# Index scores and the top-256 search two query tiles ahead, and their room reused for score rows

## The chip, the cores and the metric

The kernel runs on one core of a Trainium2 chip. The metric is the device time of one execution in microseconds (us). The engines are TensorE (PE in the profile, its weight loads PEld), VectorE (DVE), ScalarE (ACT), GpSimd (POOL) and SyncE (SP), which issues most of the DMA transfers.

## What is computed

One transformer block on 1024 tokens of width 1024: a hybrid attention, an attention to 256 memory rows, and a squared-ReLU MLP of width 4096. The hybrid attention has eight heads of dense-sparse attention (DSA), in which every query attends only to the 256 keys that an index network scores highest, and eight heads of NSA with three branches (compressed, selected, window). Cut to what the change touches:

```
idx_score = einsum('bqhs,bqh->bqs', relu(einsum('bqhd,bsd->bqhs', qi, k_i)), wi)   # 8 index heads
idx_score = where(pos <= t, idx_score, -inf)
_, sel = top_k(idx_score, 256)
s = einsum('bqhd,bqkd->bhqk', qd, k_d[sel]) * scale        # DSA: softmax over the selected keys
o_dsa = softmax(s) @ v_d[sel]
o_nsa = o_cmp * g0 + o_slc * g1 + o_win * g2               # NSA, three softmax attentions
x = x + concat(o_dsa, o_nsa) @ w_out
x = x + memory_attention(rms_norm(x));  x = x + relu(rms_norm(x) @ w_ff_in)**2 @ w_ff_out
```

The kernel does not gather the 256 keys. It finds the 256th largest index score of every query row, and adds a mask of 0 or 1e30 to the DSA scores.

## The kernel before

The 1024 queries are eight tiles of 128 rows. The program is written as Python generators, which yield after each step an amount of work `w` in the planner's own units; a scheduler then fixes the order of the instructions on every engine when the program is built, with semaphores between the engines. Each engine executes its own list in that order.

There are two streams. The **fill** (`fill`, L1100) is the projection of the second half of the tokens (`project`, part 1), the memory rows (`memory`), output projection and memory attention for tiles 0 and 1 and then 2 and 3 (`between`), the MLP of tiles 0 to 3 (`mlp`), and `between` for tiles 4 and 5. `between` reads the attention outputs of its tiles, which `finish` (L713) stored to DRAM. The **attention** (`attend`, L835) walks the query tiles t = 0 to 7. `together` (L110) merges the two: fill is taken while its sum stays under the attention's sum times a pace (1.35, later 1.75); a stage of the fill that needs the outputs of tile n is held until the attention's tile is past n; and where `attend` yields `(t, None)`, the attention is held until the next half of the projection is out, with fill alone meanwhile.

In one tile, NSA and DSA come as units: `scores` (L667) for two heads, one unit ahead of `values` (L697). `scores` puts two score matmuls into PSUM ("S", two buffers), DVE adds the mask and copies to a score row `S` in SBUF (L686), ACT takes the exponential (L688), POOL normalizes (L693). `values` transposes the row on PE (L703), ACT and DVE split it in two parts (L235, L236), and PE multiplies by V (psPV). A tag `S` has NS = 4 rows of 4 KB a partition.

`index_mask` (L600) makes the mask of one tile beside the attention of the tile before it: `beside` (L89) interleaves `tile_work(t)` with the index work in proportion. First come the index scores: for eight heads two matmuls into PSUM "S", a ReLU on ACT into `ir` (L612), a weighted sum on DVE into `isc` (L616, L618). Then the search, 32 rounds on ACT alone, each round three instructions that need each other's result:

```python
for b in range(15, -1, -1):                                   # for the high and the low 16 bits
    s.activation(mask, src, AF.Sign, bias=c, accum_out=over)  # L644: over the whole row, and the sum of it
    s.activation(step, over, AF.Sign, bias=nd)                # L645
    s.activation(c, step, AF.Identity, scale=-0.5 * (1 << b), bias=c)   # L646
    yield 0.1
```

and at its end some ten DVE instructions that make the mask (L650 to L663). `isc`, `tkh` and `tkl` have one buffer each, so the index scores of the next tile cannot be written until the search before is through. `attend` runs it one tile ahead: `index_mask(aw, st, t + 1)` in tile t; tiles 0 and 1 need no mask, so there are six searches, of tiles 2 to 7, beside tiles 1 to 6. The index keys of tiles 4 to 7 come from part 1 of the projection, so the hold for it stands before the first tile whose index work reads them.

`q_prep` (L560) loads a head group's queries from DRAM (`qin`, one DMA on SP's queue, L564), normalizes and rotates them on POOL and DVE, transposes and splits them.

Of the kernel before, what the change touches and what calls it, by code (L numbers as in the profile page):

```python
# [9 lines left out]
F32 = mybir.dt.float32  # L10
F32R = mybir.dt.float32r
# [11 lines left out]
P = 128  # L23
L = 1024
# [64 lines left out]
def beside(ga, ta, gb, tb):  # L89

    da = db = 0.0
    la = lb = True
    while la or lb:
        if la and (not lb or da * tb <= db * ta):
            w = next(ga, None)
            la = w is not None
            da += w or 0.0
        else:
            w = next(gb, None)
            lb = w is not None  # L100
            db += w or 0.0
        if w is not None:
            yield w
# [63 lines left out]
def build(nc, tc, I, C, out):  # L167
# [41 lines left out]
    def swap(x):  # L209
        return halves(x)[..., ::-1, :]  # L210

    def halves(x):
        if len(x.shape) == 2:
            return x.rearrange("p (j i) -> p j i", j=2)
        return x.rearrange("p h (j i) -> p h j i", j=2)
# [4 lines left out]
    def small(pool, tag, w, dt=F32, bufs=2, p=P):  # L220
        return pool.tile([p, w], dt, tag=tag, name=tag, bufs=bufs)
# [128 lines left out]
    nc.sync.dma_start(qg[:, 1, :], row(W["nsa_qn_g"]).to_broadcast([P, 64]))  # L350
    nc.sync.dma_start(qg[:, 2, :], W["nsa_kn_g"][0:1].to_broadcast([P, 64]))
    v.tensor_scalar(qg[:, 0:2, :], qg[:, 0:2, :], -1.0, None, op0=ALU.mult)
    qgs = at.tile([P, 3, 64], F32, tag="qgs", name="qgs")
    v.tensor_copy(halves(qgs), swap(qg))
    xqg = bcast("xqg", row(W["xq_norm_g"]), 128)
    masks = const16("c_masks", [P, 640])
    window, causal = masks[:, 0:512], masks[:, 128:640]
# [10 lines left out]
    def project(pool, part, pe, st):  # L368
# [17 lines left out]
        nc.sync.dma_start(ctab[:, 0, :], C["c_ccos"])  # L386
        nc.sync.dma_start(ctab[:, 1, :], C["c_csin"])
        v.tensor_tensor(ctab[:, 0, :], ctab[:, 0, :], qg[:, 2, :], op=ALU.mult)
        v.tensor_tensor(ctab[:, 1, :], ctab[:, 1, :], qgs[:, 2, :], op=ALU.mult)
        kg = ring(pool, "pc", [P, 8, 64])  # L390
        lnb = kg[:, 6, :]
        for h, src in enumerate([W["nsa_kn_g"][1:2], W["nsa_kn_g"][1:2], W["nsa_kn_g"][2:3], W["nsa_kn_g"][2:3],
# [164 lines left out]
    def part_of(t):  # L557
        return max(i for i, (a, _) in enumerate(PARTS) if a <= t)

    def q_prep(aw, t, kind, hg):  # L560

        q = small(aw, "qin", 256, bufs=1).rearrange("p (h d) -> p h d", d=64)
        part = part_of(t)
        nc.sync.dma_start(q, qraw[kind][part][hg][:, t - PARTS[part][0], :].rearrange("p (h d) -> p h d", d=64))  # L564
        ta = small(aw, "qta", 256, bufs=1).rearrange("p (h d) -> p h d", d=64)
        tb = small(aw, "qtb", 256, bufs=1).rearrange("p (h d) -> p h d", d=64)
        if kind == 2:
            A, B = cos[:, t, None, None, :].to_broadcast([P, 4, 2, 32]), sin[:, t, :]
        else:
            tab = small(aw, "qtab", 128, bufs=1).rearrange("p (a d) -> p a d", d=64)  # L570
            g.tensor_tensor(halves(tab[:, 0, :]), halves(qg[:, kind, :]), cos[:, t, None, :].to_broadcast([P, 2, 32]), op=ALU.mult)
            g.tensor_tensor(tab[:, 1, :], sin[:, t, :], qgs[:, kind, :], op=ALU.mult)
            A, B = halves(tab[:, 0, :])[:, None, :, :].to_broadcast([P, 4, 2, 32]), tab[:, 1, :]
            s.activation(ta, q, AF.Square)
            ss, r = small(aw, "qss", 4), small(aw, "qr", 4)
            v.tensor_reduce(ss, ta, axis=AX.X, op=ALU.add)
            g.tensor_scalar(ss, ss, 64 * EPS, None, op0=ALU.add)
            g.tensor_tensor(r, ss, mhalf[:, 0:1].to_broadcast([P, 4]), op=ALU.pow)
            g.tensor_tensor(q, q, r[:, :, None].to_broadcast([P, 4, 64]), op=ALU.mult)
        g.tensor_tensor(halves(ta), halves(q), A, op=ALU.mult)  # L580
        v.tensor_tensor(halves(tb), swap(q), halves(B)[:, None, :, :].to_broadcast([P, 4, 2, 32]), op=ALU.mult)
        qd = small(aw, "qd", 512, bufs=1).rearrange("p (h b d) -> p h b d", h=4, b=2)
        v.tensor_tensor(qd[:, :, 0, :], ta, tb, op=ALU.add)
        g.tensor_tensor(qd[:, :, 1, :], ta, tb, op=ALU.add)
        own = ("iqh", "iql", 1) if kind == 2 else ("qh", "ql", 2)
        qh = aw.tile([P, 4, P], F32R, tag=own[0], name=own[0], bufs=own[2])
        ql = aw.tile([P, 4, P], F32R, tag=own[1], name=own[1], bufs=own[2])
        p2 = pst("PT", [P, 4, P])
        for h in range(4):
            te.transpose(p2[:, h, :], qd[:, h, :, :].rearrange("p b d -> p (b d)"), ident)  # L590
        split_ps(p2, qh, ql)
        return qh, ql
# [4 lines left out]
        a = (n + 1) // 2  # L597
        return [(0, a), (a, n - a)]

    def index_mask(aw, st, t):  # L600
        Wd = (t + 1) * P
        acc = small(aw, "isc", L, bufs=1)
        for hg in range(2):
            qh, ql = q_prep(aw, t, 2, hg)
            for h in range(4):
                for c, n in chunks_of(t + 1):
                    sp = pst("S", [P, n * P])
                    mv = st["K"][:, IDX, c * P:(c + n) * P]
                    mm(sp, qh[:, h, :], mv, True, False)
                    mm(sp, ql[:, h, :], mv, False, True)  # L610
                    r = small(aw, "ir", 512)
                    s.activation(r[:, :n * P], sp, AF.Relu)  # L612
                    dst = acc[:, c * P:(c + n) * P]
                    w = st["wi"][:, t, hg * 4 + h:hg * 4 + h + 1]
                    if hg == 0 and h == 0:
                        v.tensor_scalar(dst, r[:, :n * P], w, None, op0=ALU.mult)  # L616
                    else:
                        v.scalar_tensor_tensor(dst, r[:, :n * P], w, dst, op0=ALU.mult, op1=ALU.add)  # L618
                yield 0.15 * (t + 1)
        sc = acc[:, :Wd]  # L620
        v.tensor_tensor(acc[:, t * P:Wd], acc[:, t * P:Wd], causal[:, 384:512], op=ALU.subtract)
        bits = sc.bitcast(I16).rearrange("p (n b) -> p n b", b=2)
        mask = small(aw, "dmask", L, BF16)[:, :Wd]
        sgn = mask.bitcast(I16)
        hi, lo = small(aw, "tkh", L, U16, 1)[:, :Wd], small(aw, "tkl", L, U16, 1)[:, :Wd]
        v.tensor_scalar(sgn, bits[:, :, 1], 0.0, -1.0, op0=ALU.is_lt, op1=ALU.mult)
        v.scalar_tensor_tensor(hi.bitcast(I16), sgn, -32768, bits[:, :, 1], op0=ALU.bitwise_or, op1=ALU.bitwise_xor)
        v.tensor_tensor(lo.bitcast(I16), bits[:, :, 0], sgn, op=ALU.bitwise_xor)
# [35 lines left out]
        st["dm"][t] = mask  # L664
        yield 0.1

    def scores(aw, qh, ql, K, kt0, nk, mask, gate):  # L667


        sums = small(aw, "sums", 2)  # L670
        Ss = []
        for hh in range(2):
            S = small(aw, "S", L, bufs=NS)[:, :nk * P]
            mn = small(aw, "mn", 2, bufs=4)
            for i, (c, n) in enumerate(chunks_of(nk)):
                sp = pst("S", [P, n * P])
                mv = K(kt0 + c, kt0 + c + n)
                mm(sp, qh[hh], mv, True, False)
                mm(sp, ql[hh], mv, False, True)
                dst = S[:, c * P:(c + n) * P]  # L680
                m = mask(c, n)
                low = mn[:, i:i + 1]
                if m is None:
                    v.tensor_scalar(dst, sp, 1.0, mn[:, 0:1] if i else None, op0=ALU.mult, op1=ALU.min, accum_out=low)
                else:
                    v.tensor_tensor_reduce(out=dst, in0=sp, in1=m, scale=1.0, scalar=mn[:, 0:1] if i else 3e38,  # L686
                                           op0=ALU.add, op1=ALU.min, accum_out=low)
            s.activation(S, S, AF.Exp, bias=low, scale=-1.0, accum_out=sums[:, hh:hh + 1])  # L688
            Ss.append(S)

        v.reciprocal(sums, sums)  # L691
        for hh in range(2):
            g.tensor_scalar(Ss[hh], Ss[hh], sums[:, hh:hh + 1], 1.0 if gate is None else gate[:, hh:hh + 1],  # L693
                            op0=ALU.mult, op1=ALU.mult)
        return Ss
# [15 lines left out]
                mm(pv, vv, pl[:, j], False, last and kt == nk - 1)  # L711

    def finish(aw, t, c, pv):  # L713
        oc = small(aw, "oc", 256)[0:64].rearrange("p (h q) -> p h q", h=2)
        s.activation(oc, pv[64:128], AF.Copy)
        v.tensor_tensor(oc, pv[0:64], oc, op=ALU.add)
        nc.sync.dma_start(oT_dr[t][c].rearrange("(h d) q -> d h q", h=2), oc)
# [116 lines left out]

    def attend(aw, st):  # L835

        main = attention(aw, st)
        held = []

        def of_tile(t):  # L840
            while True:
                x = held.pop() if held else next(main, None)
                if x is None:
                    return
                if x[0] > t:
                    held.append(x)
                    return
                yield x[1]
        for t in range(NT):
            if t + 1 in [a for a, _ in PARTS[1:]]:  # L850
                yield t, None
            side = index_mask(aw, st, t + 1) if 2 <= t + 1 < NT else iter(())
            for w in beside(of_tile(t), tile_work(t), side, 8 * 0.15 * (t + 2) + 3.4):
                yield t, w
        for x in main:
            yield x


    def memory(pool):
# [201 lines left out]
    def pe_stack():  # L1061
# [19 lines left out]
        "wi": at.tile([P, NT, 8], F32, tag="wi", name="wi"),  # L1081
        "gi": at.tile([P, NT, 24], F32, tag="gi", name="gi"),
        "dm": {},
        "ix": set(),
    }
    for kv in range(2):
        v.memset(st["cT"][kv], 0.0)
# [64 lines left out]
```

## Time and profile before

| what | value |
|---|---|
| time of the timed runs | 1833.72 us median of 3 (1833.55 to 1837.51) |
| profiled execution, its own time | 1835.75 us |
| its span, first to last instruction | 1833.9 us |
| mean granted clock of TensorE | 0.97 |
| busy, sum over the span | PE 1726.9, PEld 1474.2, DVE 936.1, ACT 1074.6, POOL 895.0 us |
| attention ends (last DSA output of tile 7) | near 1330 us |
| MLP of tiles 4 to 7 alone | from about 1490 us |

"Busy" is the time in which an engine executes at least one instruction. Matmuls are pipelined, so PE counts as busy in a stretch in which its matmuls come less often than they could; how often they could come is read from the start times of consecutive matmuls in a dense stretch. The granted clock is the share of its full clock that PE was given. In a list of groups, a line stands for all instructions of one source line, engine and operation, with their count, busy time and mean duration.

### The profile page before, as it was taken

How to read it: one execution, taken by the hardware profiler on the slowest of the kernel's cores; microseconds unless marked ns; L12 is line 12 of the kernel's file. 1: busy time of each engine (PE TensorE's matmuls, PEld its weight loads, DVE VectorE, ACT ScalarE, POOL GpSimd, SP SyncE). 2: the span in 40 equal slices, each digit the busy share in tenths (PEclk: the TensorE clock that was granted, in tenths of full speed). 3: DMA queues.
4: the chain of work that ended last, by engine and by line, in shares of the span. 5: the costliest groups of instructions: out<-in, count | busy, mean ns of one | idle time of the engine just before them, and what ended most of it. 6: DMA issues, size and time to landing. Idle time of an engine off the chain costs nothing. (4 is left out here: it accounts for less than half of the span.)

```text
span 1833.9 us, 28049 instructions
## 1 busy us (share of the span) xinstructions
PE 1726.9 (94%) x9262; PEld 1474.2 (80%) x9262; DVE 936.1 (51%) x2353; ACT 1074.6 (59%) x2687; POOL 895.0 (49%) x1034
## 2 busy tenths in 40 slices
PE   5996999889989998999999999999999799999999
PEld 5995988777878787778887788888988578787787
DVE  4553766575684678466664656646523422222222
ACT  4444658889588669955797457994412323333332
POOL 2364657446262244677676576662111144454443
PEclk9997998999999999999999999999989799999999
DMA  8224512256335320222112112125394222222232
GB/s 203 70 87 160 103 34 79 78 193 180 122 112 162 120 81 24 73 81 71 64 63 91 54 65 75 60 79 185 99 288 131 71 69 92 92 93 93 94 99 98
DMA packets 180081, 187.50 MB, mean 102 GB/s; under 512 B 34656, under 2 KB 149088, under 8 KB 179936
## 3 DMA queue, kind: packets, MB, share of 16 engines
q1 hardware_dynamic: 172000, 175.23, 30.8%
q0 software_dynamic: 7936, 10.49, 2.2%
q8 instruction: 73, 1.20, 0.3%
q14 instruction: 72, 0.59, 0.1%
HBM read 164.69 MB, written 20.97 MB: 101 GB/s over the span
## 5 line engine op out<-in xcount | busy, mean ns | idle before, releaser
L249 POOL TENSOR_TENSOR wlo<-wraw,whi 128x512 fp32r<-128x512 f32 (+1 forms) x230 | 308.5, 1347 | 278.7 <-ACT whi L244 247.6
L244 ACT ACTIVATE whi<-wraw 128x512 fp32r<-128x512 f32 (+2 forms) x289 | 181.1, 628 | 247.4 <-PE psS L218 147.1
L218 PE MATMUL psD<-whi,xh 128*128 128x256 f32 (+1 forms) x704 | 193.8, 359 | 3.6 <-ACT whi L244 2.9
L218 PE MATMUL psD<-wlo,xh 128*128 128x256 f32 (+1 forms) x704 | 194.8, 357 | 0.8 <-DMA wlo<-in_w_in_dram 0.8
L236 DVE TENSOR_TENSOR pl<-psPT,ph 128x512 fp32r<-128x512 f32 (+1 forms) x232 | 142.2, 621 | 78.2 <-ACT ph L235 75.4
L218 PE MATMUL psD<-whi,h 128*128 128x512 f32 x512 | 174.3, 404 | 1.8 <-POOL h L1037 1.0
L688 ACT ACTIVATE S<-S,mn 128x128 f32<-128x128 f32 (+7 forms) x192 | 142.7, 744 | 41.5 <-DVE mn L686 40.3
L218 PE MATMUL psS<-whi,h 128*128 128x512 f32 x512 | 162.1, 392 | 5.1 <-DVE b L899 5.1
L693 POOL TENSOR_SCALAR S<-S,sums,gi 128x640 f32<-128x640 f32 (+7 forms) x128 | 107.7, 850 | 106.7 <-DVE sums L691 99.0
L235 ACT ACTIVATE ph<-psPT 128x512 fp32r<-128x512 f32 (+1 forms) x232 | 122.8, 540 | 60.9 <-PE psPT L703 54.5
L249 DVE TENSOR_TENSOR wlo<-wraw,whi 128x512 fp32r<-128x512 f32 (+1 forms) x59 | 64.3, 1090 | 166.9 <-ACT whi L244 166.8
L218 PEld LDWEIGHTS psD<-whi,xh 128*128 128x128 f32 x704 | 134.0, 198 | 14.3 <-ACT whi L244 3.3
L218 PEld LDWEIGHTS psD<-wlo,xh 128*128 128x128 f32 x704 | 134.8, 197 | 12.5 <-DMA wlo<-in_w_in_dram 1.2
L703 PE MATMUL psPT<-c_ident,S 128*128 128x128 f32 x816 | 132.3, 279 | 8.3 <-DVE ql L236 4.2
L899 DVE TENSOR_TENSOR b<-psS,b 128x512 f32<-128x512 f32 (+1 forms) x80 | 50.0, 635 | 152.6 <-PE psS L218 152.6
L218 PEld LDWEIGHTS psS<-whi,h 128*128 128x128 f32 x512 | 96.1, 188 | 29.3 <-DVE b L899 9.3
L218 PE MATMUL psS<-K,qh 128*128 128x384 f32 (+3 forms) x288 | 113.5, 397 | 5.6 <-DVE mn L686 2.8
L218 PEld LDWEIGHTS psD<-whi,h 128*128 128x128 f32 x512 | 95.6, 190 | 23.7 <-DVE b L899 1.5
L703 PEld LDWEIGHTS psPT<-c_ident,S 128*128 128x128 f32 x816 | 98.1, 143 | 18.9 <-POOL S L693 5.6
L218 PE MATMUL psD<-wlo,h 128*128 128x512 f32 x256 | 102.5, 404 | 1.3 <-POOL wlo L249 1.3
L218 PE MATMUL psD<-xh,wlo 128*128 128x512 f32 x256 | 101.5, 398 | 0.0
L899 DVE TENSOR_TENSOR b<-psD,b 128x512 f32<-128x512 f32 (+1 forms) x112 | 63.2, 572 | 74.5 <-PE psD L218 73.0
(299 smaller groups left out, 4647.4 us busy)
## 6 DMA issues: line engine op xcount, KB each, us to landing
wraw<-in_w_ff_in_dram SPq DMA_DIRECT2D x128, 256.0 KB, 2.7
wraw<-in_w_ff_out_dram SPq DMA_DIRECT2D x128, 256.0 KB, 2.6
whi<-in_w_out_dram SPq DMA_DIRECT2D x32, 256.0 KB, 5.0
wlo<-in_w_out_dram SPq DMA_DIRECT2D x32, 256.0 KB, 4.6
wraw<-in_w_in_dram SPq DMA_DIRECT2D x24, 256.0 KB, 3.1
q<-st SPq DMA_DIRECT2D x12, 512.0 KB, 2.6
qin<-q SPq DMA_DIRECT2D x44, 128.0 KB, 2.3
x<-in_x_dram SPq DMA_DIRECT2D x8, 512.0 KB, 5.2
```

Source lines behind the costliest of these rows:

```text
L218: te.matmul(o, a, b, start=start, stop=stop)
L235: s.activation(hi, src, AF.Copy)
L236: v.tensor_tensor(lo, src, hi, op=ALU.subtract)
L244: s.activation(hi, raw, AF.Copy)
L249: (v if l == "v" else g).tensor_tensor(lo, raw, hi, op=ALU.subtract)
L688: s.activation(S, S, AF.Exp, bias=low, scale=-1.0, accum_out=sums[:, hh:hh + 1])
L693: g.tensor_scalar(Ss[hh], Ss[hh], sums[:, hh:hh + 1], 1.0 if gate is None else gate[:, hh:hh + 1], op0=ALU.mult, op1=ALU.mult)
L703: te.transpose(p2[:, j, hh, :], S[:, (c + j) * P:(c + j + 1) * P], ident)
L899: v.tensor_tensor(dst, pt, dst, op=ALU.add)
```

## The change

`index_mask` gets a pool of its own, `ix`, for the index queries, `isc`, `ir`, `tkh` and `tkl`, and runs two tiles ahead: the mask of tile t + 2 is made in tile t. The hold for part 1 of the projection moves one tile forward with it, from before tile 3 to before tile 2. The mask gets a third buffer. After tile 5 (the last with index work) the pool `ix` is closed and a pool `sx` opened in the same room; from then on every second call of `scores` takes its two score rows from `sx`, which also has four. `sums` and `mn` get more buffers, `oc` in `finish` one instead of two, and the swapped copy `qgs` of the query gains gives way to swapped reads of `qg`.

```diff
-    qgs = at.tile([P, 3, 64], F32, tag="qgs", name="qgs")
-    v.tensor_copy(halves(qgs), swap(qg))
...
-        v.tensor_tensor(ctab[:, 1, :], ctab[:, 1, :], qgs[:, 2, :], op=ALU.mult)
+        v.tensor_tensor(halves(ctab[:, 1, :]), halves(ctab[:, 1, :]), swap(qg[:, 2, :]), op=ALU.mult)
...
-            g.tensor_tensor(tab[:, 1, :], sin[:, t, :], qgs[:, kind, :], op=ALU.mult)
+            g.tensor_tensor(halves(tab[:, 1, :]), halves(sin[:, t, :]), swap(qg[:, kind, :]), op=ALU.mult)
...
-        qh = aw.tile([P, 4, P], F32R, tag=own[0], name=own[0], bufs=own[2])
-        ql = aw.tile([P, 4, P], F32R, tag=own[1], name=own[1], bufs=own[2])
+        qh = (ix or aw).tile([P, 4, P], F32R, tag=own[0], name=own[0], bufs=own[2])
+        ql = (ix or aw).tile([P, 4, P], F32R, tag=own[1], name=own[1], bufs=own[2])
...
-    def index_mask(aw, st, t):
+    def index_mask(aw, ix, st, t):
-        acc = small(aw, "isc", L, bufs=1)
+        acc = small(ix, "isc", L, bufs=1)
...
-                    r = small(aw, "ir", 512)
+                    r = small(ix, "ir", 512)
...
-        mask = small(aw, "dmask", L, BF16)[:, :Wd]
+        mask = small(aw, "dmask", L, BF16, 3)[:, :Wd]
-        hi, lo = small(aw, "tkh", L, U16, 1)[:, :Wd], small(aw, "tkl", L, U16, 1)[:, :Wd]
+        hi, lo = small(ix, "tkh", L, U16, 1)[:, :Wd], small(ix, "tkl", L, U16, 1)[:, :Wd]
...
+    turn = {"i": 0}
     def scores(aw, qh, ql, K, kt0, nk, mask, gate):
-        sums = small(aw, "sums", 2)
+        sums = small(aw, "sums", 2, bufs=4)
+        turn["i"] += 1
         for hh in range(2):
-            S = small(aw, "S", L, bufs=NS)[:, :nk * P]
-            mn = small(aw, "mn", 2, bufs=4)
+            S = small(st["more"] if st["more"] and turn["i"] % 2 else aw, "S", L, bufs=NS)[:, :nk * P]
+            mn = small(aw, "mn", 2, bufs=8)
...
-        oc = small(aw, "oc", 256)[0:64].rearrange("p (h q) -> p h q", h=2)
+        oc = small(aw, "oc", 256, bufs=1)[0:64].rearrange("p (h q) -> p h q", h=2)
...
     def attend(aw, st):
         main = attention(aw, st)
+        ix_pool = tc.tile_pool(name="ix", bufs=1, side="right", reuse_waits="tile")
+        ix = ix_pool.__enter__()
...
         for t in range(NT):
-            if t + 1 in [a for a, _ in PARTS[1:]]:
+            if t + 2 in [a for a, _ in PARTS[1:]]:
                 yield t, None
-            side = index_mask(aw, st, t + 1) if 2 <= t + 1 < NT else iter(())
-            for w in beside(of_tile(t), tile_work(t), side, 8 * 0.15 * (t + 2) + 3.4):
+            side = index_mask(aw, ix, st, t + 2) if t + 2 < NT else iter(())
+            for w in beside(of_tile(t), tile_work(t), side, 8 * 0.15 * (t + 3) + 3.4):
                 yield t, w
+            if t + 3 == NT:
+                ix_pool.__exit__(None, None, None)
+                more_pool = tc.tile_pool(name="sx", bufs=1, side="right", reuse_waits="tile")
+                st["more"] = more_pool.__enter__()
         for x in main:
             yield x
+        more_pool.__exit__(None, None, None)
...
-        "ix": set(),
+        "more": None,
```

More of the change, by code (lines that the diff above doesn't have):

```diff
@@ L558, in part_of, with q_prep @@
         return max(i for i, (a, _) in enumerate(PARTS) if a <= t)
-    def q_prep(aw, t, kind, hg):
+    def q_prep(aw, t, kind, hg, ix=None):
         q = small(aw, "qin", 256, bufs=1).rearrange("p (h d) -> p h d", d=64)
@@ L598, in chunks_of @@
         return [(0, a), (a, n - a)]
-    def index_mask(aw, st, t):
+    def index_mask(aw, ix, st, t):
         Wd = (t + 1) * P
-        acc = small(aw, "isc", L, bufs=1)
+        acc = small(ix, "isc", L, bufs=1)
         for hg in range(2):
-            qh, ql = q_prep(aw, t, 2, hg)
+            qh, ql = q_prep(aw, t, 2, hg, ix)
             for h in range(4):
```

## The prediction

> **What bounds the kernel now.** I read the page first, for the shares and the slices.
>
> ```profile
> span 1833.9 us, 28049 instructions
> PE 1726.9 (94%) x9262; PEld 1474.2 (80%) x9262; DVE 936.1 (51%) x2353; ACT 1074.6 (59%) x2687; POOL 895.0 (49%) x1034
> PE   5996999889989998999999999999999799999999
> ACT  4444658889588669955797457994412323333332
> PEclk9997998999999999999999999999989799999999
> ```
>
> TensorE looks full, but its busy time includes the tail of each pipelined matmul. How densely matmuls can follow each other is read from the timeline of PE, by start times:
>
> ```profile
> 1623.38 0.39 PE L218 MATMUL psS<-xl,whi 128*128 128x512 f32 x1
> 1623.61 0.39 PE L218 MATMUL psS<-xh,whi 128*128 128x512 f32 x1
> ...
> 1227.56 0.28 PE L218 MATMUL psPV<-pl,V 128*128 128x256 f32 x1
> 1227.67 0.28 PE L218 MATMUL psPV<-ph,V 128*128 128x256 f32 x1
> ...
> 1301.60 1.03 PE L703 MATMUL psPT<-c_ident,S 128*128 128x128 f32 x8
> 1302.47 0.60 PE L218 MATMUL psD<-wlo,b 128*128 128x256 f32 x2
> 1302.91 0.38 PE L218 MATMUL psD<-whi,b 128*128 128x256 f32 x1
> ```
>
> So a matmul of 512 columns takes 0.23 us of PE, one of 256 columns 0.115, a transpose 0.87 / 8 = 0.109, and a product in plain fp32, which runs as two passes, 0.44. With these (0.175 for 384 columns, 0.11 for the small ones, in proportion) all of PE's instructions add up to 1657 us. I call this PE work, and use the running sum as a ruler: "at 400" means after 400 us of PE work. On it the attention runs from about 150 to 1200. Finding the same instructions in the trace gives the time at each mark: 100, 400, 550, 700 and 1200 of PE work are passed at 127, 460, 634, 807 and 1329 us. Windows with these ends:
>
> ```profile
> core 0: us, PE busy (x) PEld busy (x) DVE busy (x) ACT busy (x) POOL busy (x), PEclk, DMA share, GB/s
> 127.00:460.00 333.00, 301.25 (x1700) 263.88 (x1699) 201.07 (x639) 242.59 (x790) 190.15 (x297) 0.93 0.41 118
> 460.00:634.00 174.00, 163.43 (x926) 140.61 (x925) 113.39 (x340) 125.58 (x341) 60.56 (x87) 0.98 0.41 127
> 634.00:807.00 173.00, 162.52 (x890) 135.70 (x889) 111.24 (x285) 134.38 (x327) 97.73 (x112) 0.99 0.22 69
> 807.00:1329.00 522.00, 514.25 (x2753) 436.55 (x2752) 303.74 (x710) 361.66 (x795) 310.91 (x315) 0.99 0.25 82
> 1070.00:1329.00 259.00, 256.62 (x1424) 221.19 (x1423) 153.11 (x378) 181.44 (x396) 138.51 (x143) 0.99 0.30 95
> 400.00:450.00 50.00, 46.70 (x263) 40.48 (x262) 30.30 (x92) 47.78 (x149) 31.09 (x47) 1.00 0.54 145
> ```
>
> Time less PE work is lost time: 33 of 333, 24 of 174, 23 of 173, 22 of 522 us. The loss is in the first half of the attention; beside the MLP, in the last long row, little can be won. What takes it is seen in the last row: there ACT, with 47.8 of 50 us, is the full engine. What fills ACT is the search, from the list of groups:
>
> ```profile
> L688 ACT ACTIVATE S<-S,mn 128x128 f32<-128x128 f32 (+7 forms) x192 | 142.7, 744 | 41.5 <-DVE mn L686 40.3 <-DVE xnb L963 0.4
> L235 ACT ACTIVATE ph<-psPT 128x512 fp32r<-128x512 f32 (+1 forms) x232 | 122.8, 540 | 60.9 <-PE psPT L703 54.5 <-PE psPV L218 2.0 <-DVE mn L686 2.0
> L644 ACT ACTIVATE dmask<-tkl,tkt 128x384 bf16<-128x384 uint16 (+5 forms) x96 | 84.3, 878 | 5.6 <-DVE tkl L642 3.8
> L644 ACT ACTIVATE dmask<-tkh,tkt 128x384 bf16<-128x384 uint16 (+5 forms) x96 | 84.2, 877 | 5.4 <-DVE tkl L628 4.3
> L646 ACT ACTIVATE tkt<-tks,tkt 128x1 f32<-128x1 f32 x192 | 55.8, 290 | 3.2
> L645 ACT ACTIVATE tks<-tko,tkg 128x1 f32<-128x1 f32 x192 | 55.5, 289 | 2.4
> L644 ACT ACTIVATION_READ_ACCUMULATOR dmask<-tkh,tkt 128x1 f32 x96 | 18.2, 190 | 0.0
> ```
>
> One round is 0.88 + 0.19 + 0.29 + 0.29 = 1.65 us, six searches of 32 rounds 317 us of instructions, more than all exponentials. ACT executes its list in order, so a score row's exponential or a split (L235) behind some rounds waits, and PE waits for the split.
>
> **The measure for the change.** The order in which the built program's instructions stand can be read for both kernels. I put each ACT and DVE instruction at the PE mark of the last PSUM result that its engine has read, gave it its mean duration from the groups of this trace, scaled so that an engine's sum is its busy time on the page (1074.6 and 936.1), and summed by 50 us of PE work. A stretch takes at least the fullest engine's time. ACT / DVE:
>
> ```
> PE work from  before   after     PE work from  before   after
> 150           42/46    47/48     600           66/45    55/44
> 200           30/37    55/31     650           39/23    48/24
> 250           58/47    41/47     700           26/31    29/29
> 300           64/44    65/34     800           52/28    40/31
> 350           56/36    24/33     850           40/26    71/22
> 400           29/42    63/53     900           24/26    13/22
> 450           58/46    64/61     1000          50/25    26/28
> 500           38/34    63/31     1050          47/25    31/27
> 550           32/45    36/58     1100          32/40    23/32
> ```
>
> For before the excess over 50 is 28 us between 100 and 400, 8 between 400 and 550, 16 between 550 and 700, 2 later: 54 of the 102 lost. The order is right; what remains are waits shorter than a stretch. Where ACT is fullest they are smallest: 250 to 400 sums to 178 and took 187 (273 to 460 us), 9 more; 400 to 550 sums to 158 and took 174, 16 more.
>
> **What the change does, part by part.** PE's, ACT's and POOL's lists hold the same instructions as before and DVE's one less (the copy `qgs`); what changes is their place.
>
> *The searches crowd together.* On the ruler they lie at 251-320, 337-399, 459-520, 601-664, 776-880 and 998-1113 before, at 186-254, 288-347, 410-452, 493-550, 611-705 and 818-898 after. Between 400 and 550 two searches stand where one stood: 32 rounds more, 32 x 1.65 x 0.865 (1074.6 of 1242 us that ACT's durations add up to) = 46 us, and 12 more exponentials and 18 more splits, 18 us: ACT goes from 124 to 191 us, against 150 of PE. Also, `attend` now holds for the projection before tile 2: the planner counts 52 units of fill alone instead of 8, and then owes the attention 38 units without fill. In the built order the fill comes out ahead, reaches the output projection of tiles 2 and 3, which needs the outputs of tile 3, and stands: from 467 to 502 PE's list has 246 matmuls of attention and index with no matmul of the fill between them (35 us of PE work against 54 of DVE and 46 of ACT); the longest such run before has 69. So this stretch takes 191 + 9 = 200 instead of 174: **+26**. At the lower end ACT's list drifts and only the excess over 150 us long stretches counts, 15 instead of 0 of which some is in the 16 already lost: +8; at the upper the chains of the run without fill add to ACT's sum: +41.
>
> *Between 100 and 400* the excess falls from 28 to 20: **-5** (0 to -8, since small waits fill in). *Between 550 and 700* from 16 to 13: **-3**.
>
> *After 700.* At 850 ACT has 71 us, the end of tile 7's search in blocks of 14 and 10 rounds, but 13 in the next 50; over the two there is no excess. I take **+5**, between 0 and 20. The mask of tile 7 no longer comes late, tiles 6 and 7 have no search beside them, and eight score rows stand in flight instead of four (by the order, 5 to 7 rows between their score matmul and their last transpose at 950 to 1200, where it was 4). But 1070 to 1329 us is 259 us for 250 of PE work: 9 us is all there is. **-5** (0 to -9). The stall at a handover of the one `isc` buffer stays, as there are still five handovers:
>
> ```profile
> 1006.47 0.50 PE L218 MATMUL psD<-whi,h 128*128 128x512 f32 x1 [0.96 <-POOL h L1037]
> 1009.01 0.30 PE L218 MATMUL psS<-Kc,qh 128*128 128x64 f32 x1 [1.34 <-ACT ir L612]
> 1013.13 0.69 PE L218 MATMUL psS<-K,qh 128*128 128x384 f32 x1 [1.50 <-DVE cmn L746]
> ```
>
> *Edits at nothing.* The index queries' `qin` loads move a tile forward on SP's queue with their POOL and DVE steps; the swapped read keeps POOL's operation; `oc` with one buffer waits for its store.
>
> ```profile
> qin<-q SPq DMA_DIRECT2D x44, 128.0 KB, 2.3
> o<-oc SPq DMA_DIRECT2D x64, 64.0 KB, 2.1
> L572 POOL TENSOR_TENSOR qtab<-c_sin,qgs 128x64 f32<-128x64 f32 x32 | 10.5, 328 | 0.0
> ```
>
> Twelve loads of 2.3 us hide, as each is issued ahead of a search of 32 x 1.65 = 53 us; the swapped read costs at most another 10.5 us of POOL, which is idle half the time; 64 stores of 2.1 us come some 18 us apart, and if two came closer ACT would stand 2 us. Together 0, at worst 3.
>
> Sum: 26 - 5 - 3 + 5 - 5 = **+18 us**. Against the profiled execution (1833.9 span, 1835.75 own time) that is 1853.8; the median of the runs is 2.0 below it, so 1852 us.
>
> **Rivals.** *The lead pays.* With two tiles of lead nobody waits for the masks, so ACT's backlog at 400 to 550 is worked off in the emptier stretches (350 has 24 us of ACT) and the fill covers PE. Then 8 - 5 - 3 + 0 - 10 = -10: 1824 us. For it: the late stage is clearly emptier. Against it: ACT's order is fixed at build, so rounds cannot step aside. It decides if the stretch 400 to 550 takes under 180 us. Chance 0.18.
>
> *The run without fill lowers the clock.* The granted clock falls where PE has gaps, as in these two windows:
>
> ```profile
> 145.00:200.00 55.00, 40.47 (x221) 34.89 (x221) 28.01 (x107) 27.09 (x89) 33.41 (x58) 0.81 0.66 165
> 1004.00:1014.00 10.00, 5.68 (x19) 3.68 (x20) 9.82 (x14) 3.06 (x8) 7.49 (x6) 0.76 0.15 52
> ```
>
> At half clock 35 us of PE work become 70, over DVE's 54: +15, so 1867 us. Against it: of 400 to 450, an ACT-bound window, the clock is 1.00. Chance 0.12. [...]
>
> *The moves cancel.* 191 is absorbed to about 180 and the late part gives its 9: within 3 us, 1834. Chance 0.07. That the change doesn't do what it says is excluded by the order.
>
> **The numbers.** The forecast has 0.63. 0.2% (4 us) is about what a measurement of this kernel can tell from no change. Slower: 0.63 and 0.12, faster 0.18, same 0.07. Bounds of the terms: low -10, high 41 - 3 + 20 = +58 with everything bad; a range from 1828 to 1878 leaves out about one in ten at each side.
>
> **What would show it.** Right: in after, the PE time between the end of the first output projection and tile 3's last output has a stretch of some 55 to 65 us with matmuls of attention alone and DVE and ACT near full; 400 to 550 of PE work takes about 200 us; from the MLP's start to the attention's end nearly no loss. Wrong: that stretch passes in under 180 us, or the rounds of two searches run there without PE gaps.

## The result and the profile after

The changed kernel takes 1911.5 us (median of 4 runs, 1910.53 to 1912.81) against 1835.28 us (1833.55 to 1837.51) for the kernel before beside it: ratio 1.0415, 95% interval 1.0397 to 1.0433. It is 76 us slower; forecast were 18. The profiled execution took 1910.68 us. Its page, the same rows as shown of before:

```profile
span 1908.9 us, 28068 instructions
PE 1749.3 (92%) x9262; PEld 1483.2 (78%) x9262; DVE 933.0 (49%) x2352; ACT 1080.3 (57%) x2687; POOL 888.8 (47%) x1034
PE   5996999879977988899999999999989889999999
ACT  4444794973886976896559965564431233333332
PEclk9998998989998989999999999999999789999999
```

The work of every engine is what it was: 9262 matmuls, 2687 ACT instructions, ACT busy 1080 against 1075 us. So what has grown is waiting. A slice is 47.7 us here; PE has a 7 in slices 9, 12 and 13, that is from 382 to 430 and from 525 to 620 us, where before had no digit under 8 between the fifth slice and the end of the attention.

On the ruler of PE work the marks 100, 400, 550, 700 and 1200 are passed at 125, 477, 699, 874 and 1396 us (before: 127, 460, 634, 807, 1329). The windows between them, then the one from mark 1200 to mark 1350, and as the last row the same of before:

```profile
core 0: us, PE busy (x) PEld busy (x) DVE busy (x) ACT busy (x) POOL busy (x), PEclk, DMA share, GB/s
125.00:477.00 352.00, 305.35 (x1646) 262.63 (x1645) 191.80 (x588) 226.18 (x740) 164.95 (x257) 0.93 0.41 119
477.00:699.00 222.00, 181.75 (x996) 150.64 (x995) 138.37 (x391) 186.40 (x510) 85.23 (x130) 0.92 0.31 93
699.00:874.00 175.00, 161.37 (x878) 138.08 (x878) 111.20 (x301) 136.97 (x329) 93.90 (x106) 0.95 0.19 60
874.00:1396.00 522.00, 512.52 (x2748) 433.47 (x2746) 286.48 (x698) 321.34 (x681) 310.06 (x319) 1.00 0.26 82
1396.00:1591.00 195.00, 174.70 (x805) 145.75 (x806) 60.91 (x140) 50.74 (x107) 38.99 (x44) 0.89 0.42 133
...
1329.00:1517.00 188.00, 171.16 (x807) 143.98 (x806) 61.75 (x143) 51.75 (x111) 40.19 (x46) 0.90 0.44 139
```

From 100 to 400 of PE work the kernel takes 352 us instead of 333, from 400 to 550 it takes 222 instead of 174, then 175 instead of 173, 522 as before, and from 1200 to 1350 it takes 195 instead of 188. So 48 of the 75 us lie in one stretch, the one the prediction named. What PE waits for there, after first and then before (us in total, times, longest):

```profile
engine line waited for: us in total, times, longest us
PE psS L218 <- ACT ir L610: 13.1, 1, 13.1
PE psM L274 <- DMA relu<-xo: 4.7, 1, 4.7
```

```profile
PE psM L274 <- DMA relu<-xo: 3.0, 1, 3.0
PE psM L274 <- ACT xh L278: 1.4, 2, 0.7
```

One wait of 13.1 us for `ir`, the ReLU of the index scores, is new. The timeline around it, in after, first of PE, then of ACT, then of DVE:

```profile
526.12 0.62 PE L218 MATMUL psS<-K,iql 128*128 128x384 f32 x2
530.72 0.34 PE L218 MATMUL psS<-K,iql 128*128 128x384 f32 x1
565.50 1.03 PE L218 MATMUL psD<-wlo,b 128*128 128x256 f32 x4
579.59 0.42 PE L218 MATMUL psS<-Kc,qh 128*128 128x64 f32 x1 [13.06 <-ACT ir L610]
...
526.79 0.85 ACT L610 ACTIVATE ir<-psS 128x384 f32<-128x384 f32 x2
573.05 0.29 ACT L644 ACTIVATE tkt<-tks,tkt 128x1 f32<-128x1 f32 x1
579.04 0.87 ACT L610 ACTIVATE ir<-psS 128x384 f32<-128x384 f32 x2 [5.69 <-DVE isc L614]
...
574.35 0.88 DVE L655 TENSOR_SCALAR_CACHE_REDUCE dmask<-isc,tkb 128x640 bf16<-128x640 f32 x1
575.74 1.49 DVE L658 TENSOR_TENSOR_SCAN isc<-tkh 128x640 f32<-128x640 bf16 x1
577.27 0.88 DVE L659 SCALAR_TENSOR_TENSOR tkh<-isc,tkc,tkh 128x640 bf16<-128x640 f32 x1
578.60 0.74 DVE L614 TENSOR_SCALAR isc<-ir,wi 128x384 f32<-128x384 f32 x2
```

From 489 to 573 us ACT runs the search of tile 4 (its last round ends with the row at 573.05). In the midst of it PE does index scores of tile 5: of one head at 524 to 526, which the ReLU brings into the two buffers of `ir` at 526.79, and of a second at 529.83 to 530.72, which stay in PSUM. There they stay: the ReLU needs `ir`, `ir` is read by the weighted sum (L614), and that writes `isc`, which until 578.2 belongs to the search of tile 4, whose end compares it with the threshold (L655) and uses it as room for the prefix sum (L658, L659). The rounds themselves read only `tkh` and `tkl`. PSUM "S" has two buffers, and the second head has both. So from 530.7 to 579.6 no score of the attention can be made either: the attention stands still for 49 us. Fill covers PE to 566.5, and then there is none left to put there.

Such a standstill is nothing new. In before, at the handover between the same tiles:

```profile
577.11 0.33 PE L218 MATMUL psS<-K,iql 128*128 128x384 f32 x1
...
620.66 0.38 PE L218 MATMUL psS<-Kc,qh 128*128 128x64 f32 x1
```

It has 44 us without a score, and PE did fill. The windows of the two standstills, before and after, with the columns as above:

```profile
577.00:620.60 43.60, 40.85 (x198) 35.52 (x197) 18.37 (x48) 33.06 (x87) 6.14 (x8) 0.96 0.57 186
```

```profile
531.00:579.60 48.60, 28.51 (x145) 24.21 (x144) 17.61 (x45) 35.67 (x97) 8.22 (x13) 0.83 0.40 119
```

All five handovers, named by the tile whose index scores stand in PSUM; the standstill goes from the last of these matmuls to the next score matmul, and PE's idle time is the length of that window less PE busy in it (all rounded, the sums after adding):

```
                      tile 3   tile 4   tile 5   tile 6   tile 7    sum
before   standstill     25       23       44       44       44      180 us
         PE idle         5        0        3        2        3       12
after    standstill     24       40       49       51       46      210
         PE idle         5       12       20        9        3       49
```

The standstills are 30 us longer; PE's idle time in them is 37 us more, as the fill no longer covers them. At the third the fill is out of work because it needs the attention: what comes next in it loads outputs of tile 3, and each of these loads is issued 2 to 4 us behind the store of an `oc`. The last such pair before the fill's next matmul, and that matmul:

```profile
630.82 0.59 SPq L718 DMA_DIRECT2D o<-oc  x1
632.89 0.33 SPq L917 DMA_DIRECT2D b<-o  x1
...
635.31 0.59 PE L218 MATMUL psD<-whi,b 128*128 128x256 f32 x2
```

So the attention stood for the search and the fill then stood for the attention: between the fill's last matmul (566.15) and its next (635.31) lie 69 us, 13 of them the gap and 56 the run of 246 matmuls of attention and index, which are 35 us of PE work.

### The profile page after: what moved, and what is told of

Same layout as the page of the kernel before. It is cut to its first block, busy times and chain, and to the rows that moved or that the text cites. A ratio compares the mean times of both kernels' runs of the same rounds, so it can differ in the third digit from the quotient of the medians.

```text
span 1908.9 us, 28068 instructions
## 1 busy us (share of the span) xinstructions
PE 1749.3 (92%) x9262; PEld 1483.2 (78%) x9262; DVE 933.0 (49%) x2352; ACT 1080.3 (57%) x2687; POOL 888.8 (47%) x1034
## 5 line engine op out<-in xcount | busy, mean ns | idle before, releaser
L218 PE MATMUL psS<-xh,whi 128*128 128x512 f32 x256 | 101.8, 399 | 0.0
```

The costliest lines, as they stand in the source:

```text
L218: te.matmul(o, a, b, start=start, stop=stop)
```

## Experiments

Three theories stood at the beginning. T1 is the forecast's own: ACT is crowded where two searches stand, so time goes with ACT's sum. T2: the handovers of the one `isc`, held through the search, keep back the next index scores and what stands behind them. T3: the moved hold before tile 2 lets the fill get ahead by itself, and it is missing later. Lost time (time less PE work, in us) by stretches of PE work, for the profiled execution of every run that is used below:

```
                          100-250 250-400 400-550 550-700 700-950 950-1200 1200-1350
before                       -4      37      24      23      13       9        38
after                         0      51      72      26      16       6        45
e1  after, light              0      44      37      33       9      14        22
e2  before, light            -5      31      17      32       8      10        27
e3  after, isc free           0      35      25      32      11       7        25
e4  before, isc free         -3      36      15      32      10      12        26
e5  after, isc held          -1      47      72      26      20       6        44
e6  lead 2 for 2 and 3        0      37      23      26      14      16        46
e7  after, no more rows       0      51      72      28      10      18        22
e8  before, free, exact      -4      36      17      33       8      14        31
e9  before, small edits      -5      30      27      28      10       7        37
e10 one tile ahead, rows     -5      31      25      28      12      18        51
e11 after, free, exact        0      35      30      29      13       8        24
e12 e11 without rows          1      36      32      27       4      11        27
```

**e1 and e2: shorter search rounds.** The search instructions of ACT work on 128 elements instead of up to 1024, and one count on DVE with them, so the threshold found is one of the first 128 keys and the mask is another; the number of rounds and their place stay. e1 is after, e2 is before with the same edit.

```diff
...
-                s.activation(mask, src, AF.Sign, bias=c, accum_out=over)
+                s.activation(mask[:, 0:P], src[:, 0:P], AF.Sign, bias=c, accum_out=over)
```

> The changed kernel with every search round on 128 columns instead of the whole row (it then finds the median of the first 128 keys, not the 256th of all): a round's first ScalarE instruction falls from 0.6-1.15 us to about 0.3, its place and its chain of three stay. Read beside the same edit of the kernel before. Theory 1 (ScalarE is too full where two searches stand in the place of one): most of the 76 us go, this kernel comes to within 25 us of the kernel before with the same edit. Theory 2 (at the hand-over of the one isc buffer TensorE waits for the end of the search before): the searches end earlier, so most of it goes too. Theory 3 (the fill is held and owed, and runs out of work; the run of attention without fill): the order of the fill is as it was, so over 40 us between the two stay.

> The kernel before with every search round on 128 columns (the same edit). All theories: faster than the kernel before, as its own excess of ScalarE goes; some 15 to 40 us of the 102 lost, so 1795 to 1820 us.

Measured: e1 1848.08 us, ratio 1.0082 (1.0053 to 1.0111); e2 1816.78 us, 0.9909 (0.9893 to 0.9925). The gap between the two kernels shrinks from 76 to 31 us, which lies between the bounds of T1 (under 25) and T3 (over 40) and meets neither. Some of it lives on with a search that is lighter on ACT (in before an exponential of 128 elements takes 0.40 us on ACT, L688, a round's first instruction 0.61 to 1.14 us, L644), so ACT's sum is not all of it. But a shorter search also gives `isc` back earlier: the standstills over 12 us behind index scores are 14, 17, 35 and 22 us in e1 and 16, 23, 28 and 31 in e2. So the two runs do not decide between T1 and T2.

**e3, e4 and e5: `isc` released or held.** In e3 (after) and e4 (before) the end of the search compares the high halves in `tkh` and puts the prefix sum in the room of `tkl`, so that `isc` is free once the halves are split off; the low halves are left out of the mask. e5 is the control: after with the same comparisons, but the sum still in `isc`.

```diff
-        v.tensor_scalar(mask, sc, thf, None, op0=ALU.is_gt, op1=ALU.add, accum_out=cnt)
+        v.tensor_scalar(mask, hi, low, None, op0=ALU.is_gt, op1=ALU.add, accum_out=cnt)   # e3, e4, e5
-        v.tensor_scalar(eq, sc, thf, None, op0=ALU.is_equal)
+        v.tensor_scalar(eq, hi, low, None, op0=ALU.is_equal)                              # e3, e4, e5
-        v.tensor_tensor_scan(sc, eq, eq, 0.0, op0=ALU.add, op1=ALU.bypass)
+        cs = lo.bitcast(BF16)                                                             # e3, e4
+        v.tensor_tensor_scan(cs, eq, eq, 0.0, op0=ALU.add, op1=ALU.bypass)
...
```

> The changed kernel with isc free as soon as the 16-bit halves are made: the mask is taken from the high halves alone (the low half's threshold is still searched for but not used), so the search no longer holds isc until its end. Theory 2: TensorE's gap of 13 us at 566 us and the smaller ones like it go, 15 to 35 us faster than the changed kernel. Theories 1 and 3: within 8 us of the changed kernel, as no work leaves ScalarE and the fill is as it was.

> The kernel before with isc free early, the same edit. Theory 2: it too loses something at its five hand-overs, 3 to 10 us faster than the kernel before. Theories 1 and 3: within 4 us of it.

> A control for the run with isc free: the same two comparisons on the 16-bit high halves at the search's end, but the running count is written to isc and read from it as in the changed kernel, so isc is held until the search is through. Theory 2 (the held isc is the cause): as slow as the changed kernel, 1895 to 1925 us. If the cheaper comparisons, or the luck of another built order, made the gain: 1825 to 1850 us.

Measured: e3 1831.43 us, ratio 0.9983 (0.9968 to 0.9997); e4 1825.42, 0.9956 (0.9942 to 0.9970); e5 1909.99, 1.0397 (1.0379 to 1.0415). Between e3 and e5 only the place of the prefix sum differs, and with it its type (bf16 for f32), which costs DVE nothing: the six sums take 10.5 us in e3 and 10.6 in e5. It is worth 0.0414 of the time of before, 76 us, as much as the whole loss. So the hold of `isc` is shown as the cause, with index work two tiles ahead: in before the same release (e4) is worth 8 us. T2 had the side right and e3's size wrong: it forecast 15 to 35 us from the gap and others like it, and against after 80 came. The stretch from 400 to 550 of PE work in e3, then in e5, and the first waits of PE in e3's:

```profile
464.00:639.00 175.00, 165.93 (x944) 143.59 (x943) 127.85 (x357) 152.81 (x417) 78.03 (x112) 0.96 0.39 118
```

```profile
473.00:695.00 222.00, 181.23 (x993) 148.83 (x992) 136.99 (x388) 186.43 (x508) 81.16 (x126) 0.93 0.31 94
```

```profile
PE psS L218 <- DVE mn L688: 2.4, 4, 1.4
PE psD L218 <- DMA b<-o: 2.1, 2, 1.8
```

In e5 the stretch has the 222 us of after, and standstills of 23, 33, 49, 51 and 50 us. In e3 it has 175, no wait for `ir` is among its largest, and not one stretch without scores over 12 us begins behind index scores. One thing speaks against reading e3 as a wait taken away and nothing else: the order of instructions is fixed at build by a scheduler that knows when a buffer is free. With `isc` free it lays ACT's list otherwise: by the sum made for the prediction, ACT has 159 us of instructions between 400 and 550 in e3, 192 in e5 and 191 in after, and the longest run of PE without fill is 48 matmuls, against 246 in e5 and after. So most of the crowding that the prediction saw is itself a result of the held buffer. Which part of the 76 us is order and which is waiting on the chip, these runs do not separate.

They also put T3 down as a cause by itself: e3 still has the hold before tile 2 and passes the mark 400 at 464 us, before at 460. Whether the moved hold adds to the loss while `isc` is held is open, as no run moves it alone.

**e6: lead of two for tiles 2 and 3 only.** The index work of tile 2 runs in tile 0, of tile 3 in tile 1, and from tile 4 on one tile ahead as in before; the hold stands as in before.

```diff
-            if t + 2 in [a for a, _ in PARTS[1:]]:
+            if t + 1 in [a for a, _ in PARTS[1:]]:
...
-            side = index_mask(aw, ix, st, t + 2) if t + 2 < NT else iter(())
+            n = {0: 2, 1: 3, 3: 4, 4: 5, 5: 6, 6: 7}.get(t)
+            side = index_mask(aw, ix, st, n) if n else iter(())
...
-            if t + 3 == NT:
+            if t + 2 == NT:
```

> The changed kernel with the two tiles of lead for tiles 2 and 3 alone (their index work in tiles 0 and 1, none in tile 2, then one tile ahead as before), so that the hold for the projection stands before tile 3 again; the pools and the extra score rows (for tile 7) stay. Theory 2: the index work has its old room from tile 4 on and more before, so within 15 us of the kernel before, 1820 to 1850 us. Theory 3 (the hold): the same. If the new pools and small edits alone cost: over 1860 us.

Measured: 1859.39 us, ratio 1.0127 (1.0104 to 1.0149), slower than expected. Up to 700 it loses 6 us more than before. Of the 22 us by which its profiled execution is longer, 15 are lost late: 7 more from 950 to 1200 and 8 more from 1200 to 1350, beside and after tile 7. That pointed to the one part that acts only there, the score rows.

**e7 and e10: the score rows.** e7 is after without the additional rows; e10 is after with index work and hold one tile ahead as in before, so that it holds the rows, the small edits and the pool `ix` alone.

```diff
e7
-            S = small(st["more"] if st["more"] and turn["i"] % 2 else aw, "S", L, bufs=NS)[:, :nk * P]
+            S = small(aw, "S", L, bufs=NS)[:, :nk * P]
e10
...
-            side = index_mask(aw, ix, st, t + 2) if t + 2 < NT else iter(())
+            side = index_mask(aw, ix, st, t + 1) if 2 <= t + 1 < NT else iter(())
...
-            if t + 3 == NT:
+            if t + 2 == NT:
```

> The changed kernel without the extra score rows: every score row is from the four old ones. All theories: the rows are worth 0 to 9 us in tiles 6 and 7, so 1911 to 1921 us.

> The kernel before with the small edits, the pool of its own for the index work (still one tile ahead) and the extra score rows, which then serve tile 7 alone. The prediction's view (rows help or do nothing): 1828 to 1836 us. The view from the run without rows: in the built order the attention then ends at 1215 of PE work instead of 1200, less of the work after it has fill beside it, and 5 to 20 us are lost after the attention's end: 1840 to 1855 us.

Measured: e7 1896.09 us, ratio 1.0319 (1.0299 to 1.0338), 14 us below its neighbour e5 and below the 1911 to 1921 that every theory gave it; e10 1854.45, 1.0102 (1.0078 to 1.0126). More rows cost time in either arrangement: 14 us by e5 less e7, 22 by e10 less e9 (below), in which the pool `ix` is contained. e6 has these rows too, and e10's loss is nearly as large as its own. The timeline of DVE in after shows how; L685 and L687 make a score row in two parts, L661 is the last instruction of the mask of tile 7:

```profile
1047.41 0.47 DVE L687 CUSTOM_DVE_ANT_0 S<-psS,c_masks,mn 128x256 f32<-128x256 f32 x1
...
1118.67 0.43 DVE L661 TENSOR_SCALAR dmask<-dmask 128x1024 bf16<-128x1024 bf16 x1
1119.02 0.68 DVE L685 TENSOR_SCALAR_CACHE_REDUCE S<-psS 128x512 f32<-128x512 f32 x1
1119.74 0.62 DVE L687 CUSTOM_DVE_ANT_0 S<-psS,c_masks,mn 128x384 f32<-128x384 f32 x1
```

For 72 us there is no score row at all. The rows of `sx` lie where `tkh`, `tkl` and `isc` of the last search lie, and the first call of `scores` that is given one has to wait for the end of that search; in the order as built it stands behind that end, with the calls after it, though those have rows of the old kind. Without the additional rows (e7) the same 72 us hold nine rows. Each ends with an instruction of the first line here; five have their first part in the second line, four on L685:

```profile
L687 DVE CUSTOM_DVE_ANT_0 S<-psS,c_masks,mn x9: 468/484/618, 1050.9 to 1108.2; 128x256 f32<-128x256 f32 x5, 128x384 f32<-128x384 f32 x4
L687 DVE CUSTOM_DVE_ANT_0 S<-psS,c_masks x5: 546/557/558, 1050.1 to 1107.5; 128x384 f32<-128x384 f32 x5
```

The windows of these 72 us, after and e7, and of the like place in e10, where no row is made from 1172.8 to 1236.9 us, and e9 (before with the small edits, without rows):

```profile
1048.00:1120.00 72.00, 68.63 (x318) 53.72 (x317) 28.44 (x52) 57.71 (x130) 41.63 (x40) 1.00 0.24 76
```

```profile
1048.00:1120.00 72.00, 72.00 (x400) 61.71 (x399) 39.64 (x107) 66.14 (x159) 45.88 (x50) 1.00 0.22 68
```

```profile
1174.00:1240.00 66.00, 60.48 (x273) 47.27 (x273) 27.26 (x53) 48.30 (x111) 37.11 (x33) 0.97 0.27 86
```

```profile
1174.00:1240.00 66.00, 66.00 (x362) 56.18 (x361) 34.53 (x91) 59.20 (x143) 44.34 (x45) 1.00 0.24 74
```

Meanwhile PE is not empty: it does fill, 68.63 of 72 us in after. This is a sixth standstill, behind the search of tile 7, which in before hands its buffers to nobody. That is why the loss does not show at its place (950 to 1200: 6 us). It shows later: the attention ends later, and, as I read the order, the fill that ran meanwhile is not there to cover its end. The last output of the attention (`oc`) and what follows, after and then e7:

```profile
L717 DVE TENSOR_TENSOR oc<-psPV,oc x64: 393/415/418, 188.2 to 1400.8; 64x256 f32<-64x256 f32 x64
```

```profile
L717 DVE TENSOR_TENSOR oc<-psPV,oc x64: 394/412/418, 188.5 to 1370.9; 64x256 f32<-64x256 f32 x64
1406.00:1578.00 172.00, 161.83 (x816) 137.46 (x815) 63.39 (x154) 56.33 (x119) 40.45 (x45) 0.95 0.37 114
```

The attention ends at 1401 us in after and at 1371 in e7, and the stretch from 1200 to 1350 of PE work takes 195 us against 172.

**e9: the small edits alone.** Before, with the buffer counts of the mask, `sums`, `mn` and `oc` and the swapped reads.

```diff
...
-        mask = small(aw, "dmask", L, BF16)[:, :Wd]
+        mask = small(aw, "dmask", L, BF16, 3)[:, :Wd]
...
-        oc = small(aw, "oc", 256)[0:64].rearrange("p (h q) -> p h q", h=2)
+        oc = small(aw, "oc", 256, bufs=1)[0:64].rearrange("p (h q) -> p h q", h=2)
```

> The kernel before with the small edits alone: swapped reads of qg instead of qgs, a third mask buffer, more buffers for sums and mn, oc with one. Every theory, and the prediction's 'edits at nothing': 0 to 3 us, 1834 to 1837 us; anything beyond shows what another built order alone does.

Measured: 1831.96 us, ratio 0.9983 (0.9973 to 0.9994): 3 us less, against 0 to 3 more in the forecast.

**e8, e11 and e12: `isc` free with the whole result.** The comparisons are made on both halves, so that the mask is the same; e8 is before, e11 after, e12 after without the additional rows.

```diff
...
+        v.tensor_scalar(lwl, th[:, 1:2], -1.0, None, op0=ALU.mult)
+        v.tensor_scalar(mask, hi, low, None, op0=ALU.is_gt, op1=ALU.add, accum_out=cnt)
+        v.tensor_scalar(eq, hi, low, None, op0=ALU.is_equal)
+        v.scalar_tensor_tensor(mask, lo, lwl, mask, op0=ALU.is_gt, op1=ALU.add)
+        v.tensor_reduce(c2, mask, axis=AX.X, op=ALU.add)
+        v.scalar_tensor_tensor(eq, lo, lwl, eq, op0=ALU.is_equal, op1=ALU.mult)
+        v.tensor_scalar(cnt, c2, -1.0, float(TOPK), op0=ALU.mult, op1=ALU.add)
+        cs = lo.bitcast(BF16)
+        v.tensor_tensor_scan(cs, eq, eq, 0.0, op0=ALU.add, op1=ALU.bypass)
+        v.scalar_tensor_tensor(eq, cs, cnt[:, 0:1], eq, op0=ALU.is_le, op1=ALU.mult)
...
```

> The kernel before with isc free early and the whole result: the mask is made of both 16-bit halves (greater in the high half, or equal there and greater in the low one, and the first of the ties), two more VectorE instructions a tile than the run on high halves alone. Theory 2: 4 to 10 us faster than the kernel before, 1824 to 1831 us. Otherwise 1834.

> The changed kernel with isc free early and the whole result (mask of both 16-bit halves). Theory 2: as the run with isc free, 1826 to 1840 us, so the lead of two tiles itself neither gains nor costs over 6 us against the kernel before with the same edit (1830.5).

> The same without the extra score rows. If the rows cost as they did in the changed kernel (15 us): 1812 to 1826 us. If they cost only where they move the attention's end (here it stands at 1175 of PE work with and without them): within 5 us of the run with rows.

Measured: e8 1830.53 us, ratio 0.9965 (0.9951 to 0.9979); e11 1838.06, 1.0015 (1.0003 to 1.0027); e12 1831.56, 0.9990 (0.9974 to 1.0006). e8 came as forecast; e11 is in its range, but not within 6 us of e8 (0.0050 of the time, 9 us); e12 misses its first forecast and lies 5 to 7 us from e11, near its second. With these the loss can be laid out. Holding `isc` costs 1.0319 - 0.9990, some 60 us, with what it does to the order, once the index work runs two tiles ahead (e7 less e12). The rows cost 14 to 18 us with `isc` held (after or e5 less e7) and 5 to 7 with it free (e11 less e12). The lead itself, with `isc` free and without rows (and with the small edits, worth 3 us by e9), is 0.9990 against 0.9965, with intervals that just overlap: it brings nothing. The version to keep is e8, 6 us faster than before and 81 faster than after: the release of `isc` without any of the change. Its stretch from 400 to 550 takes 167 us where before took 174:

```profile
459.00:626.00 167.00, 159.87 (x926) 139.92 (x925) 117.36 (x324) 127.55 (x353) 59.31 (x90) 0.99 0.45 138
```

## Why the prediction was wrong in size

The side was right and the time was not: 1911.5 us lie above the whole range (1828 to 1878).

*The step that failed: "The stall at a handover of the one `isc` buffer stays, as there are still five handovers."* It counted the handovers and took their size from PE's waits in before, 1.34 us in the row shown. That was the price under cover. The handover itself was a standstill of the attention of 23 to 44 us even in before, which the fill hid (12 us idle in 180); the step named no work that hides it and put no price on the case without that work. In after three of the five are covered badly (12, 20 and 9 us idle). The control pair e3 and e5 prices the hold at 76 us, e7 and e12 at 60; the term in the sum was 0. With the hold goes the order that it brings about, and the two are not separated.

*Between 400 and 550: +26, 8 to 41; measured +48.* ACT's sum came out: 191 us of instructions were forecast, the window shows 186.40 busy. So did the run without fill, 56 us against 55 to 65, and it is there for the reason given, the outputs of tile 3; the gap of 13 us before it was not foreseen. What did not hold is that the time is ACT's sum and 9 to 16 us of small waits. For e3 that gives 168 to 175, and 175 were measured; for after it gives 200 to 207, and 222 were measured. Of the 15 to 22 us more, 13.06 are the gap, in which PE does nothing.

*Between 100 and 400: -5; measured +19.* The sign was wrong. The excess of ACT did fall, but two handovers lie here, that of tile 4 with 40 us of standstill and 12 idle where before had 23 and 0. Those 12 us are half of the 24 between forecast and measurement; the rest is open. With `isc` free (e3) mark 400 is passed at 464 us instead of 477 (473 in the control e5).

*Between 550 and 700: -3; measured +2. From 700 to 1200: +5 and -5; measured 0.* The first is 5 us off. The second agrees as a sum, but its term for the rows is not borne out: from 700 to 1200 after loses 22 us against 28 without the rows (e7), but e10 loses 30 against 17 without them (e9).

*The rows: 0 to -9; measured +14 to +18.* The prediction asked how many rows are in flight and not when the first of them is free. The room of the search is free when the search ends, near 1119 us, and for the 72 us before that no row was made. This showed outside the stretches that the prediction priced: no term stood for the time after the attention's end, and 7 us more than in before (23 more than in e7) are lost there.

*The edits at nothing* were right, with 3 us to the good (e9). *The hold before tile 2*, which the prediction feared for its 52 units of fill, costs nothing that shows where `isc` is free (e3, e11).

*The rival with the clock* (+15 more) had the run without fill at half clock. That did not happen. The gap, the run behind it, the stretch of low clock that begins in the gap, and the rest of the run, in after:

```profile
566.50:579.60 13.10, 0.04 (x2) 0.02 (x1) 6.04 (x18) 6.99 (x20) 0.00 (x0) 0.64 0.08 31
579.60:635.30 55.70, 47.20 (x246) 34.28 (x247) 47.94 (x126) 43.69 (x116) 31.79 (x45) 0.93 0.08 22
570.10:583.70 13.60, 4.09 (x12) 2.99 (x13) 9.41 (x28) 5.56 (x17) 1.38 (x2) 0.50 0.00 0
584.00:631.00 47.00, 38.52 (x212) 26.96 (x211) 41.30 (x109) 37.49 (x97) 26.92 (x38) 1.00 0.06 18
```

The clock is 0.50 from inside the gap to 4 us behind it, and 1.00 in the 47 us of the run that follow. The 15 us took half clock for all of the run, which no run shows: the run has 0.93 over its 55.70 us, and the 0.50 of the third row holds for 13.60 us, with PE busy 4.09 of them.

From 477 to 699 the clock is 0.92 where before had 0.98 from 460 to 634. If the rest of the clock were all taken from PE work, that would be 0.08 x 222 = 18 us against 0.02 x 174 = 3, and 0.36 x 13 = 5 of the 18 fall in the gap, where there is no work to lose: 10 us of the 48 at most, by this estimate. With `isc` free (e3, 464 to 639 us) the stretch has 0.96. How many of the 10 it really cost is open, as no run changed the clock and nothing else.

*"The lead pays"* is refuted for the kernel as built, and the range had left this rival out: 1824 us lies below 1828, with a chance of 0.18 where the text counts one in ten. Even with both obstacles away (e12 against e8) two tiles of lead bring nothing: what the attention waited for at the handovers was PSUM, not the masks.

## What to carry to other kernels

A stall that costs nothing in the profile may be a long one under cover: look for stretches in which one stream issues nothing at all (here no score matmul for 44 us), ask which buffer it stands for, and price the change by what covers that stretch afterwards. Room taken over from another stage was free only when the last reader of that stage was through (here near 1119 us, after 72 us without a score row), so its first user should come well after that. And try the release by itself first: a search end that no longer touches `isc` brought 6 us without any lead.

## What the hardware showed

The granted clock of after was 0.92 in the stretch with the 13 us gap (477 to 699 us, PE busy 181.75 of 222 us) and 1.00 from 874 to 1396 us, where PE is busy 512.52 of 522 us; with `isc` free (e3) the stretch had 0.96, PE busy 165.93 of 175 us. It was also 0.50 where there was no long gap. In before, at a handover where no gap between matmuls is over 1.5 us, PE is busy 2.90 of 5.20 us at a clock of 1.00, then 2.68 of 4.70 us at 0.50:

```profile
1004.00:1009.20 5.20, 2.90 (x12) 1.75 (x12) 5.17 (x4) 1.70 (x3) 5.20 (x4) 1.00 0.16 56
1009.30:1014.00 4.70, 2.68 (x9) 1.82 (x9) 4.56 (x11) 1.37 (x5) 2.19 (x3) 0.50 0.13 47
```
